# Moving row loads to GpSimd's queue, weight sums into the heads, and cover tiles across the gate pairs in a hybrid decoder layer

## The chip, the cores and the metric

The kernel runs on one core of one Trainium2 chip. The metric is the device time of one execution in microseconds (us), taken as the median of several runs. Each profile shows one execution. TensorE does the matmuls (PE in the profile, with its weight loads as PEld), VectorE is DVE, ScalarE is ACT, GpSimd is POOL, SyncE is SP. SP, ACT and POOL issue DMAs, and each of these queues is worked off in order.

## The reference

One layer of a decoder over 1024 tokens with 16 learned tokens ahead of them, in float32, model width 1024. Its mixing block projects the normalized input once and feeds two branches and two gates:

```python
proj = h @ w_in + b_in
(g_q, g_k, g_v, g_r, g_lr, m_q, m_k, m_v, m_o, m_i, m_f, gate_a, gate_b) = split(proj)
o_gla = head_rms(gla_chunked(g_q * dk**-0.5, g_k, g_v, log_a)) * silu(g_r)        # 4 heads
mq, mk = split(silu(causal_dwconv(concat(m_q, m_k))))
o_ml  = head_rms(mlstm_chunked(mq * dk**-0.5, mk, m_v, m_i, log_sigmoid(m_f))) * sigmoid(m_o)   # 4 heads
y = sigmoid(gate_a) * (o_gla @ w_branch_gla) + sigmoid(gate_b) * (o_ml @ w_branch_ml)
h = h + y @ w_out
u = causal_dwconv(rms_norm(h) @ w_up); gate, up = split(u)
h = h + (silu(gate) * up) @ w_down      # width 2816
out = rms_norm(h)[16:]
```

## The kernel before

Every float32 operand is split into a rounded high part and a low part (tile names end in H and L, or `wH`, `wL`), and a product is three matmuls: high by high, high by low, low by high. ACT makes the high part, DVE the low part. A weight tile of 512 KB takes one SP load into a raw buffer (two of them), one ACT copy and one DVE subtraction, in `prep` (L99 to L108), up to two tiles ahead of its use.

The kernel is a chain of stages. The order on each engine comes from a scheduler that takes the instructions in program order, shifted by priorities (`hp`), as its model of the time finds them ready; on the chip each engine and each queue then keeps that order.

*Heads* (`gla` and `mlstm`, L595 and L788). For s = 0 to 7 the projections of a head are the main work (`main`), and after each piece of a projection `advance` (L916) takes one step of the side work: the closing of a finished head (`post`, L544: scaling, transposes, norm, a store to `osc`) and the next step of the oldest open head. Between the fourth and the fifth head stands `small_rows` (L483), which prepares the gate rows of the second kind of head; each `yield` in it is one step. At the end of `post` of heads 3 to 6 `token_sums` (L459) builds four combinations of blocks of the normalized input on POOL and stores them to `tsc`. Heads 4 to 7 are the ones with convolutions. Tiles with the tag `gst` share one buffer.

*Tail and cover.* `merge_gate_b(j)` (L450) projects one 128-channel row block of the second merge gate with plain products and stores it to `gscb` from ACT's queue. Blocks 0, 1 and 2 (TAIL) run while the last head is closed. Block 3 (COVER) runs while `token_blocks` (L1059) loads the combinations and splits them.

*Pairs.* Thirteen pairs of row blocks (output gates of both branches, first merge gate, and the blocks of the second one that are left) are computed by `piece` (L960), two pieces each, with a Strassen-like scheme: seven products instead of eight, from the combinations and from sums of weight blocks. The results of a pair go into the row tiles `gu0` (tag `u0`, two buffers) and `gu1` (tag `u1`, one buffer). `gate_finish` (L1089) of the first eight pairs multiplies them with the heads' rows in `go` tiles (tag `o`, two buffers) and stores the product to `otd`; of the later pairs it stores the rows to `gsc` from ACT's queue. From pair 8 on (`q >= NK`), the two `o` buffers serve `half_sums`.

*Half sums.* The down projection at the end of the kernel also uses combinations of blocks of `w_down`. `half_sums` (L1103) makes one of 22 parts: two loads of 256 KB, four subtractions and two stores of 256 KB, all on POOL and its queue. Ten parts run in the pairs, five in the first branch (three after j = 1 in Y5 to Y7, two after j = 3 in Y6 and Y7), seven in the second (in Y0 to Y6).

*End tiles.* Blocks 6 and 7 of the second merge gate (END) run after the pairs as plain products.

*Branches.* The pool of the pairs is closed and `r2` takes its memory: a tile of `r2` waits for the old tiles that it lies on. `load_o` (L1162) loads eight rows of a branch's input (`ogL`, `omL`), and ACT and DVE split them (L1172, L1173). `merge_tile(j)` (L1201) loads a row of the first merge gate (`yg`) into Yj. All of it goes through SP's queue. `prod3` (L1181) multiplies: eight output blocks j for the GLA branch (`bg`), then eight for the mLSTM branch (`bm`), each of 72 matmuls into one of two groups of three PSUM banks; the first two `bg` blocks go row by row of the input as it arrives. DVE multiplies a block with the sigmoid of its gate (L1214), which frees the banks.

*Output projection and feed-forward.* `hacc` tiles h1 to h8 take the residual input in Y0 to Y7 (L1262 to L1268, all from SP); the products with `w_out` (`po`) are added to them (L1467). `hlo` (L1470) belongs to the two rows ahead of token 0. The rest of the kernel (second norm, up and down projection) is not touched.

Of the kernel before, what the change touches and what calls it, by code (L numbers as in the profile page):

```python
# [45 lines left out]
def hybrid_kernel(ctx, tc, x, meta, norm_mix, w_in, b_in, gla_w_gate, gla_b_gate, gla_norm,  # L46
# [167 lines left out]

    uk, uq, uv, ugb = {}, {}, {}, {}

    TAIL, COVER, END = (0, 1, 2), (3,), (6, 7)

    def head_units(s):
        h, g, k, q = s % 4, "gm"[s // 4], (O_GK, O_MK)[s // 4], (O_GQ, O_MQ)[s // 4]  # L220
# [149 lines left out]
    def cc(i):  # L370
        return col[:, i:i + 1]
# [99 lines left out]
            nc.sync.dma_start(tsc[i, k], src)  # L471


    raw_s = hd.tile([P, T], F32, name="raw_s", tag="raw", bufs=1)
    tcol = hd.tile([P, NC + 1, 4, 4], F32, name="tcol")

# [6 lines left out]
    def small_rows():  # L483
# [38 lines left out]
        nc.vector.tensor_tensor(d[:, :NM - 1], a[:, :NM - 1], M[:, NM - 2:NM - 1].to_broadcast([4, NM - 1]), OP.subtract)  # L522
        nc.scalar.activation(st[96:100, :NM - 1], d[:, :NM - 1], AF.Exp)
        nc.vector.memset(tcol[:, 0], 1.0)
        yield
        yield
        yield
        for g in range(3):
            tp = ps.tile([P, 4, P], F32, name=f"rtp{g}", tag="s", bufs=3)
            tq = tp.rearrange("p n (q w) -> p n q w", w=32)  # L530
# [13 lines left out]
    def post(s, o, om, sc, ncols):  # L544

        h = s % 4
        g = "g" if s < 4 else "m"
        for c in range(NC):
            nc.scalar.activation(o(c), o(c), AF.Copy, scale=sc[:, c + 1:c + 2])
        scaled = nc.scalar.activation(om, om, AF.Copy, scale=sc[:2, 0:1])  # L550
        for _ in range(3 if s != 3 else 5):
            yield
        for j in range(2):
            of = hd.tile([P, T], F32, name=f"of{s}_{j}", tag="r", bufs=2)
            for gi in range(2):
                tp = ps.tile([P, 4, P], F32, name=f"ot{s}_{j}_{gi}", tag="s", bufs=3)
                for i in range(4):
                    nc.tensor.transpose(tp[:, i, :], o(4 * gi + i)[:, j * P:(j + 1) * P], ident)
                a, b = 2 + 512 * gi, 2 + 512 * (gi + 1)
                nc.scalar.activation(of[:, a:b], tp.rearrange("p n w -> p (n w)"), AF.Copy, scale=ncols[j])  # L560
                if gi == 0:
                    yield
            tp = ps.tile([P, 4, P], F32, name=f"otm{s}_{j}", tag="s", bufs=3)
            nc.tensor.transpose(tp[:, 0, :2], om[:, j * P:(j + 1) * P], ident[:2, :2])
            nc.vector.tensor_scalar(of[:, 0:2], tp[:, 0, :2], ncols[j], None, OP.mult)
            nc.sync.dma_start(osc[g][2 * h + j], of[:, :NP])
            yield
        if 3 <= s < 7:
            with tc.issue_after(scaled.ins):
                token_sums(s - 3)  # L570

# [358 lines left out]
                advance()  # L930


    NP2 = NJ // 2
    tdn = [dram.tile([NP2, P, 2, 512], F32, name=f"tdn{i}") for i in range(2)]

    main(key_query_proj(0))
    decay(0)
    for s in range(8):
# [145 lines left out]
    def places():  # L1084

        for i in range(2):
            go[0, i] = row(f"go0_{i}", "o", 2)

    def gate_finish(q):  # L1089
        for i, u in enumerate(gu.pop(q)):  # L1090
            _, c, f, g, j = GATES[2 * q + i]
            if f is None:
                nc.scalar.dma_start(gsc[g][j], u[:, :NP])
                continue
            o = go[q, i] if q == 0 else row(f"go{q}_{i}", "o", 2)
# [5 lines left out]
    half = [(m, c) for m in range(NP2) for c in range(2)]  # L1101

    def half_sums(pool, tag, bufs=1):  # L1103
        m, c = half.pop(0)
        t = pool.tile([P, T], F32, name=f"ts{m}{c}", tag=tag, bufs=bufs)[:, :D].rearrange("p (i n) -> p i n", i=4)
        for k in range(2):
            nc.gpsimd.dma_start(t[:, 2 * k:2 * k + 2], w_dn[P * (2 * m + k):P * (2 * m + k + 1), :].rearrange(  # L1107
                "p (i n) -> p i n", i=2)[:, :, 256 * c:256 * c + 256])
        for o, a, b in ((0, 1, 0), (1, 3, 1), (3, 3, 0), (2, 2, 3)):
            nc.gpsimd.tensor_tensor(t[:, o], t[:, a], t[:, b], OP.subtract)  # L1110
        for i in range(2):
            nc.gpsimd.dma_start(tdn[i][m][:, :, 256 * c:256 * c + 256], t[:, 2 * i:2 * i + 2])
# [5 lines left out]
    with hp(PRI_W):  # L1118
        for _ in range(3):
            weights_step(0)  # L1120
    for j in COVER:
        main(merge_gate_b(j, gate_bank(f"pc{j}")))
    u2 = wp.tile([P, T], F32, name="gu2", tag="gst", bufs=1)[:, :2 * W0].rearrange("p (a b) -> p a b", b=W0)
    behind_ = None
    for q in range(NG):
        gu[q] = [row(f"gu{i}{q}", f"u{i}", 2 - i) for i in range(2)]
        for p in range(2):
            g = piece(psG, f"g{q}", p, gu[q], u2, WP[q], gate_block)
            next(g)
# [12 lines left out]
            next(g)  # L1142
            behind_ = g
        if q >= NK:
            for _ in range(2):
                half_sums(gs, "o", 2)
    next(behind_)
    for j in END:
        ugb[j] = u_cm(w_in, O_GB + P * j, f"gb{j}")
    gate_finish(NG - 1)  # L1150
    for i, j in enumerate(END):
        main(merge_gate_b(j, gate_bank(f"pe{j}"), row(f"gb{j}", "u0", 2) if i else None))
    gs_ctx.close()


# [3 lines left out]
    ps2_ctx = ctx.enter_context(ExitStack())  # L1159
    ps2 = ps2_ctx.enter_context(tc.tile_pool(name="ps2", bufs=1, space=PSUM, reuse_waits="tile"))  # L1160

    def load_o(g, pool, tags):  # L1162

        t = {}
        for p in "HL":
# [2 lines left out]
                t[p, i] = pool.tile(shape, F32R, name=f"o{g}{p}{i}", tag=tag)  # L1168
        for k in range(NK):
            h, l = (t[p, k // 4][:, k % 4, :NP] for p in "HL")  # L1170
            nc.sync.dma_start(l.bitcast(F32), otd[g][k])
            nc.scalar.activation(h, l.bitcast(F32), AF.Copy)  # L1172
            nc.vector.tensor_tensor(l, l.bitcast(F32), h.bitcast(F32), OP.subtract)  # L1173
        return tuple([t[p, k // 4][:, k % 4, :] for k in range(NK)] for p in "HL")
# [25 lines left out]

    def merge_tile(j):  # L1201
        yg.append(r2.tile([P, T], F32, name=f"yg{j}", tag=f"Y{j}")[:, :NP])
        nc.sync.dma_start(yg[j], gsc["a"][j])

    merge_tile(0)
    og = load_o("g", r2, "O")
    for j in range(NK):
        y = yg[j]
        if j < NK - 1:
            merge_tile(j + 1)  # L1210
        nc.scalar.activation(y, y, AF.Sigmoid, bias=cc(C_GA + j))
        pt = prod3(ubg[j], og, j < 2, f"bg{j}")
        with hp(PRI_E):
            merged = nc.vector.tensor_tensor(th(y), pt, th(y), OP.mult)  # L1214
        if j in (1, 3):
            with tc.issue_after(merged.ins):
                for i in (5, 6, 7) if j == 1 else (6, 7):
                    half_sums(r2, f"Y{i}")
    om_ = load_o("m", r1b, "R")

    yH = [r2.tile([P, NK, 2, 256], F32R, name=f"yH{i}", tag=f"OH{i}") for i in range(2)]
    yL = [r2.tile([P, NK, 2, 256], F32R, name=f"yL{i}", tag=f"OL{i}") for i in range(2)]
# [7 lines left out]
    for j in range(NK):  # L1230
# [17 lines left out]
                nc.scalar.activation(yh, z, AF.Copy)  # L1248
                nc.vector.tensor_tensor(yL[i][:, j], z, yh.bitcast(F32), OP.subtract)  # L1249
        if half:  # L1250
            half_sums(r2, f"Y{j}")
    r1b_ctx.close()
    ps2_ctx.close()
    psF = ctx.enter_context(tc.tile_pool(name="psF", bufs=1, space=PSUM, reuse_waits="tile"))
# [7 lines left out]
    for t in range(NC + 1):  # L1262
        a = r2.tile([P, T], F32, name=f"h{t}", tag=f"Y{t - 1}") if t else rb.tile([P, T], F32, name="h0", tag="T12")
        if t == 0:
            nc.sync.dma_start(a[:2, :D], meta[T0:NM, :])
        else:
            nc.sync.dma_start(a[:, :D], x[P * (t - 1):P * t, :])
# [545 lines left out]
```

## Time and profile before

| | |
|---|---|
| median of 3 runs | 1961.98 us (1961.19 to 1962.24) |
| the profiled execution | 1960.93 us, of which 1959.2 us span from the first to the last instruction |
| granted TensorE clock, mean | 0.985 |
| busy: PE, PEld, DVE, ACT, POOL | 96%, 91%, 61%, 44%, 19% |
| DMA | 270.03 MB, mean 138 GB/s |

The busy share of PE is a share of time in which some matmul was in flight. What a stage loses is seen in two ways: idle time ahead of an instruction with the operation that ended it, and the number of matmuls in a stretch against that in an undisturbed one, which counts a slower clock too. In the tables of stretches, the number behind x is how many instructions started in the stretch, and PEclk is the granted clock as a share of full speed.

### The profile page before, as it was taken

What the parts mean: (1) busy time and instruction counts of PE and PEld (TensorE: products, weight loads), DVE (VectorE), ACT (ScalarE), POOL (GpSimd) and SP (SyncE); (2) the same over time, 40 slices, a digit from 0 to 9 for tenths busy, and PEclk for the clock granted to TensorE, in tenths of its full rate; (3) what the DMA queues carried; (4) which work ended last, traced back from release to release, by engine and by line L of the source; (5) the groups of instructions that cost most, each with busy time, mean ns of one, the idle gap of its engine ahead of it and who ended that gap; (6) DMA issues with size and microseconds to landing.
All of it is one profiled execution on the core that took longest, in us unless ns stands there. A gap on an engine that the chain in (4) does not pass through costs nothing. (4 is left out here: it accounts for less than half of the span.)

```text
span 1959.2 us, 32654 instructions
## 1 busy us (share of the span) xinstructions
PE 1876.5 (96%) x13377; PEld 1791.5 (91%) x13377; DVE 1187.0 (61%) x1775; ACT 857.1 (44%) x1369; POOL 372.8 (19%) x405
## 2 busy tenths in 40 slices
PE   8999999899999999999679998999999999999998
PEld 8989989899999999999679998999999999987776
DVE  6555636644442666654331443688887878786776
ACT  5354554644454434322430223553434444355573
POOL 3101101122130010174330340002223222200000
PEclk9999999999999999999889999999999999999999
DMA  5111011142222675676861453333333333378794
GB/s 163 33 36 57 24 55 57 35 110 90 82 81 87 173 180 144 173 215 203 257 211 50 151 205 127 111 113 108 108 118 118 104 103 109 113 275 316 281 376 159
DMA packets 222593, 270.03 MB, mean 138 GB/s; under 512 B 13486, under 2 KB 176832, under 8 KB 222443
## 3 DMA queue, kind: packets, MB, share of 16 engines
q1 hardware_dynamic: 206651, 217.80, 35.6%
q0 software_dynamic: 11648, 39.89, 6.4%
q10 hardware_dynamic: 4144, 10.26, 1.4%
q8 instruction: 105, 1.72, 0.4%
q14 instruction: 45, 0.37, 0.1%
HBM read 198.33 MB, written 69.57 MB: 137 GB/s over the span
## 5 line engine op out<-in xcount | busy, mean ns | idle before, releaser
L1189 PE MATMUL bg<-ogH,wH_bg 128*128 128x342 f32 x192 | 63.3, 331 | 27.0 <-ACT ogH L1172 15.8
L1110 POOL TENSOR_TENSOR ts<-ts 128x256 f32<-128x256 f32 x88 | 73.7, 845 | 49.3 <-DMA ts<-in_ffn_w_down_dram 45.6
L1460 PE MATMUL po<-wH_wo,yH 128*128 128x256 f32 x256 | 73.9, 289 | 7.5 <-ACT hlo L1470 6.3
L1373 POOL TENSOR_TENSOR SB<-SA,rg 128x512 f32<-128x512 f32 x20 | 32.1, 1605 | 235.9 <-issue 114.1
L201 PE MATMUL pv<-wH_gv,xH 128*128 128x256 f32 x256 | 75.4, 294 | 0.0
L201 PE MATMUL pv<-wH_mv,xH 128*128 128x256 f32 x256 | 74.7, 292 | 0.1
L1460 PE MATMUL po<-wL_wo,yH 128*128 128x256 f32 x256 | 73.2, 287 | 0.9 <-DVE wL_wo L107 0.9
L1460 PE MATMUL po<-wH_wo,yL 128*128 128x256 f32 x256 | 73.0, 286 | 0.8 <-DVE yL L1249 0.8
L201 PE MATMUL pv<-wH_gv,xL 128*128 128x256 f32 x256 | 72.0, 281 | 0.0
L201 PE MATMUL pv<-wH_mv,xL 128*128 128x256 f32 x256 | 72.0, 281 | 0.0
L201 PE MATMUL pv<-wL_mv,xH 128*128 128x256 f32 x256 | 72.0, 281 | 0.0
L201 PE MATMUL pv<-wL_gv,xH 128*128 128x256 f32 x256 | 71.9, 281 | 0.0
L1408 DVE SCALAR_TENSOR_TENSOR cv<-u,fc,cv 128x1024 f32<-128x1024 f32 x44 | 65.3, 1484 | 0.4
L1189 PE MATMUL bg<-ogL,wH_bg 128*128 128x342 f32 x192 | 63.4, 332 | 1.1 <-DVE ogL L1173 1.1
L1107 POOL DMA_DIRECT2D ts<-in_ffn_w_down_dram x44 | 31.6, 723 | 167.2 <-DVE yM L1245 95.2
L1189 PEld LDWEIGHTS bg<-ogH,wH_bg 128*128 128x128 f32 x192 | 37.7, 197 | 27.5 <-ACT ogH L1172 16.1
L1189 PE MATMUL bg<-ogH,wL_bg 128*128 128x342 f32 x192 | 62.6, 327 | 0.0
L1355 POOL TENSOR_TENSOR A<-u2raw,A 128x512 fp32r<-128x512 f32 x20 | 43.9, 2194 | 92.9 <-ACT A L1354 92.9
L1189 PE MATMUL bm<-omH,wH_bm 128*128 128x342 f32 x192 | 61.4, 320 | 0.0
L1189 PE MATMUL bm<-omH,wL_bm 128*128 128x342 f32 x192 | 61.3, 319 | 0.0
L1189 PE MATMUL bm<-omL,wH_bm 128*128 128x342 f32 x192 | 61.2, 319 | 0.0
L675 POOL TENSOR_TENSOR pk<-pk,kT 128x256 f32<-128x256 f32 (+1 forms) x24 | 29.5, 1231 | 163.4 <-ACT pk L673 163.4
(747 smaller groups left out, 7436.0 us busy)
## 6 DMA issues: line engine op xcount, KB each, us to landing
gw<-in_w_in_dram SPq DMA_DIRECT2D x26, 512.0 KB
ts<-in_ffn_w_down_dram POOLq DMA_DIRECT2D x44, 256.0 KB, 5.2
tdn<-ts POOLq DMA_DIRECT2D x44, 256.0 KB, 2.6
rg<-in_ffn_w_up_dram SPq DMA_DIRECT2D x22, 512.0 KB
ru<-in_ffn_w_up_dram SPq DMA_DIRECT2D x22, 512.0 KB
adr<-s SPq DMA_DIRECT2D x40, 256.0 KB
rd<-in_ffn_w_down_dram SPq DMA_DIRECT2D x20, 512.0 KB
do<-tdn SPq DMA_DIRECT2D x18, 512.0 KB
```

Source lines behind the costliest of these rows:

```text
L201: nc.tensor.matmul(pt[:, :DV], a[:, k, t0:t0 + P], b[:, k % 4, :], start=(i == 0), stop=(i == 3 * NK - 1))
L675: eng.tensor_tensor(e, e, k, OP.mult)
L1107: nc.gpsimd.dma_start(t[:, 2 * k:2 * k + 2], w_dn[P * (2 * m + k):P * (2 * m + k + 1), :].rearrange("p (i n) -> p i n", i=2)[:, :, 256 * c ...
L1110: nc.gpsimd.tensor_tensor(t[:, o], t[:, a], t[:, b], OP.subtract)
L1189: nc.tensor.matmul(pt[:, i, :n], a[:, k, :], b[k][:, t0:t0 + n], start=(k == 0 and j == 0), stop=(k == NK - 1 and j == 2))
L1355: eng.tensor_tensor(l, src, h.bitcast(F32), OP.subtract)
L1373: late.tensor_tensor(sb[:, 0:4], sa[:, 0:4], rg[:, 0:4], OP.subtract)
L1408: nc.vector.scalar_tensor_tensor(y, u[:, j:SEQ + j], fc[:, j, jj:jj + 1], y, OP.mult, OP.add)
L1460: nc.tensor.matmul(pt[:, :DV], a, b[:, k % 4, :], start=(k == 0 and i == 0), stop=(k == NK - 1 and i == len(terms) - 1))
```

## The change

- Of `half_sums`, eight parts move into the heads: two at the end of `post(3)`, three each at the end of `post(4)` and `post(5)`, in the buffer `gst`. In the pairs six are left (two at pair 8, one at each later pair) in the one buffer `o0`; in the first branch three (after j = 1); in the second five, in Y0, Y1, Y2, Y2 and Y3.
- `small_rows` has six empty steps ahead of its transposes instead of three.
- COVER is blocks 3 and 4, END is block 7; blocks 5 and 6 go into the pairs. The number of pairs and of plain blocks stays the same. Block 4 uses a row of the tag `u0`, and so does block 7.
- The `o` buffers are named `o0` and `o1`; `gu1` of pairs 9 and 11 uses `o1`, so that from pair 8 on it has two buffers in turn.
- The loads of `og` and of all `yg` rows are issued from POOL's queue. The load of `om` stays on SP's, stands in the program behind block j = 1 of the first branch, and its ACT copies come behind the sigmoid of that block.
- h3, h4, h7 and h8 are loaded from POOL's queue.
- Two `issue_after` frames around POOL's work go away. They order only instructions on the named instruction's own engine, ACT or DVE, of which the framed work has none.

```diff
-    TAIL, COVER, END = (0, 1, 2), (3,), (6, 7)
+    TAIL, COVER, END = (0, 1, 2), (3, 4), (7,)
...
# small_rows
-        yield
-        yield
-        yield
+        for _ in range(6):
+            yield
...
# post
         if 3 <= s < 7:
-            with tc.issue_after(scaled.ins):
-                token_sums(s - 3)
+            token_sums(s - 3)
+            for _ in range((2, 3, 3, 0)[s - 3]):
+                half_sums(wp, "gst")
...
# places, gate_finish: rows "o" (2 buffers) become "o0" and "o1"
-            go[0, i] = row(f"go0_{i}", "o", 2)
+            go[0, i] = row(f"go0_{i}", f"o{i}")
...
-    for j in COVER:
-        main(merge_gate_b(j, gate_bank(f"pc{j}")))
+    for i, j in enumerate(COVER):
+        main(merge_gate_b(j, gate_bank(f"pc{j}"), row(f"gb{j}", "u0", 2) if i else None))
...
     for q in range(NG):
-        gu[q] = [row(f"gu{i}{q}", f"u{i}", 2 - i) for i in range(2)]
+        gu[q] = [row(f"gu0{q}", "u0", 2), row(f"gu1{q}", "o1" if q >= NK and q % 2 else "u1")]
...
         if q >= NK:
-            for _ in range(2):
-                half_sums(gs, "o", 2)
+            for _ in range(2 if q == NK else 1):
+                half_sums(gs, "o0")
...
-    for i, j in enumerate(END):
-        main(merge_gate_b(j, gate_bank(f"pe{j}"), row(f"gb{j}", "u0", 2) if i else None))
+    for j in END:
+        main(merge_gate_b(j, gate_bank(f"pe{j}"), row(f"gb{j}", "u0", 2)))
...
-    def load_o(g, pool, tags):
+    def load_o(g, pool, tags, queue):
...
-            nc.sync.dma_start(l.bitcast(F32), otd[g][k])
+            queue.dma_start(l.bitcast(F32), otd[g][k])
...
     def merge_tile(j):
-        nc.sync.dma_start(yg[j], gsc["a"][j])
+        nc.gpsimd.dma_start(yg[j], gsc["a"][j])

     merge_tile(0)
-    og = load_o("g", r2, "O")
+    og = load_o("g", r2, "O", nc.gpsimd)
     for j in range(NK):
...
-        nc.scalar.activation(y, y, AF.Sigmoid, bias=cc(C_GA + j))
+        opened = nc.scalar.activation(y, y, AF.Sigmoid, bias=cc(C_GA + j))
         pt = prod3(ubg[j], og, j < 2, f"bg{j}")
         with hp(PRI_E):
-            merged = nc.vector.tensor_tensor(th(y), pt, th(y), OP.mult)
-        if j in (1, 3):
-            with tc.issue_after(merged.ins):
-                for i in (5, 6, 7) if j == 1 else (6, 7):
-                    half_sums(r2, f"Y{i}")
-    om_ = load_o("m", r1b, "R")
+            nc.vector.tensor_tensor(th(y), pt, th(y), OP.mult)
+        if j == 1:
+            with tc.issue_after(opened.ins):
+                om_ = load_o("m", r1b, "R", nc.sync)
+            for i in (5, 6, 7):
+                half_sums(r2, f"Y{i}")
...
         if half:
-            half_sums(r2, f"Y{j}")
+            half_sums(r2, f"Y{j if j < 3 else 3 - j % 2}")
...
-            nc.sync.dma_start(a[:, :D], x[P * (t - 1):P * t, :])
+            (nc.gpsimd if t in (3, 4, 7, 8) else nc.sync).dma_start(a[:, :D], x[P * (t - 1):P * t, :])
```

More of the change, by code (lines that the diff above doesn't have):

```diff
@@ L471, in token_sums, with half_sums @@
             nc.sync.dma_start(tsc[i, k], src)
+    NP2 = NJ // 2
+    tdn = [dram.tile([NP2, P, 2, 512], F32, name=f"tdn{i}") for i in range(2)]
+    half = [(m, c) for m in range(NP2) for c in range(2)]
+    def half_sums(pool, tag, bufs=1):
+        m, c = half.pop(0)
+        t = pool.tile([P, T], F32, name=f"ts{m}{c}", tag=tag, bufs=bufs)[:, :D].rearrange("p (i n) -> p i n", i=4)
+        for k in range(2):
+            nc.gpsimd.dma_start(t[:, 2 * k:2 * k + 2], w_dn[P * (2 * m + k):P * (2 * m + k + 1), :].rearrange(
+                "p (i n) -> p i n", i=2)[:, :, 256 * c:256 * c + 256])
+        for o, a, b in ((0, 1, 0), (1, 3, 1), (3, 3, 0), (2, 2, 3)):
+            nc.gpsimd.tensor_tensor(t[:, o], t[:, a], t[:, b], OP.subtract)
+        for i in range(2):
+            nc.gpsimd.dma_start(tdn[i][m][:, :, 256 * c:256 * c + 256], t[:, 2 * i:2 * i + 2])
     raw_s = hd.tile([P, T], F32, name="raw_s", tag="raw", bufs=1)
@@ L549, in post @@
             nc.scalar.activation(o(c), o(c), AF.Copy, scale=sc[:, c + 1:c + 2])
-        scaled = nc.scalar.activation(om, om, AF.Copy, scale=sc[:2, 0:1])
+        nc.scalar.activation(om, om, AF.Copy, scale=sc[:2, 0:1])
         for _ in range(3 if s != 3 else 5):
@@ L930, in main @@
                 advance()
-    NP2 = NJ // 2
-    tdn = [dram.tile([NP2, P, 2, 512], F32, name=f"tdn{i}") for i in range(2)]
     main(key_query_proj(0))
@@ L1094, in gate_finish @@
                 continue
-            o = go[q, i] if q == 0 else row(f"go{q}_{i}", "o", 2)
+            o = go[q, i] if q == 0 else row(f"go{q}_{i}", f"o{i}")
             nc.gpsimd.dma_start(o[:, :NP], osc[g][j])
@@ L1099, in gate_finish @@
             nc.gpsimd.dma_start(otd[g][j], o[:, :NP])
[L1101 to L1112, printed above, removed]
     def gate_bank(name):
```

## The prediction, made before the changed kernel was run

> **What bounds the kernel now.** I read the page first, then the waits of TensorE, then stretches around the longest of them, then the queues in those stretches.
>
> ```profile
> span 1959.2 us, 32654 instructions
> PE 1876.5 (96%) x13377; PEld 1791.5 (91%) x13377; DVE 1187.0 (61%) x1775; ACT 857.1 (44%) x1369; POOL 372.8 (19%) x405
> ```
> ```profile
> PE bg L1189 <- ACT ogH L1172: 15.8, 1, 15.8
> PE bg L1189 <- DVE yg L1214: 11.2, 1, 11.2
> PE po L1460 <- ACT hlo L1470: 6.3, 1, 6.3
> PE Yg L957 <- DVE gu L985: 6.3, 5, 3.0
> PE rtp L534 <- ACT of L560: 4.9, 1, 4.9
> ```
>
> TensorE is the bound: it works 96% of the span, and no matmul is added or taken away by the change. So only its gaps can move, and five groups of waits (total, times, longest) make up most of them. Next, the same places as stretches of time, with two undisturbed ones (985 to 1010 and 1195 to 1210) as the measure.
>
> ```profile
> 385.00:395.00 10.00, 5.08 (x28) 4.65 (x27) 8.31 (x19) 7.61 (x9) 0.10 (x1) 0.83 0.61 173
> 400.00:590.00 190.00, 189.39 (x1314) 178.45 (x1313) 88.87 (x196) 88.67 (x177) 47.75 (x31) 1.00 0.30 86
> 865.00:880.00 15.00, 12.03 (x79) 11.83 (x78) 5.45 (x9) 2.87 (x5) 10.56 (x14) 0.77 0.90 220
> 945.00:980.00 35.00, 18.16 (x97) 16.48 (x97) 16.46 (x13) 17.96 (x18) 16.69 (x20) 0.76 0.96 317
> 985.00:1010.00 25.00, 25.00 (x160) 25.00 (x159) 1.23 (x1) 2.99 (x3) 11.88 (x17) 1.00 0.62 197
> 1010.00:1030.00 20.00, 8.75 (x42) 8.51 (x41) 13.04 (x11) 9.56 (x10) 0.00 (x0) 0.66 0.64 223
> 1180.00:1195.00 15.00, 8.69 (x52) 8.58 (x52) 2.55 (x5) 2.96 (x8) 0.00 (x0) 0.77 0.56 175
> 1195.00:1210.00 15.00, 15.00 (x127) 14.83 (x127) 5.06 (x9) 4.71 (x13) 0.00 (x0) 1.00 0.23 71
> ```
>
> The columns are length, busy time of PE, PEld, DVE, ACT and POOL with the number of instructions, PEclk, DMA share and GB/s. Undisturbed, branch matmuls start at 160/25 = 6.4 per us and the smaller ones at 127/15 = 8.47. What a stretch loses is its length less its matmuls over that rate:
>
> - A, 945 to 980: 35 − 97/6.4 = 19.8 us (15.8 of it idle, the rest slow clock and pacing by arriving rows).
> - B, 1010 to 1030: 20 − 42/6.4 = 13.4 us (11.2 idle).
> - C, 1180 to 1195: 15 − 52/8.47 = 8.9 us (6.3 idle).
> - D, 385 to 395: 10 − 28/8.47 = 6.7 us (4.9 idle).
> - E, 865 to 880: 15 − 79/8.47 = 5.7 us (3.0 idle).
>
> Together 54.5 us. A gap costs more than its idle time: PEclk is 0.66 to 0.83 in these stretches and 1.00 in the others.
>
> **A: the first branch waits for its input.** SP's queue in order of time, and the wait inside the `ogL` issues:
>
> ```profile
> 946.76 0.81 SPq L1171 DMA_DIRECT2D omL<-otdm  x2
> 948.95 0.38 SPq L102 DMA_DIRECT2D wr_bg<-in_w_branch_gla_dram  x1
> 949.39 1.18 SPq L1203 DMA_DIRECT2D yg<-gsca  x1
> 950.74 9.68 SPq L1171 DMA_DIRECT2D ogL<-otdg  x8
> 961.38 36.55 SPq L1203 DMA_DIRECT2D yg<-gsca  x6
> 998.03 0.38 SPq L102 DMA_DIRECT2D wr_bg<-in_w_branch_gla_dram  x1
> ```
> ```profile
> SPq L1171 <- PE pe L158: 4.7, 1, 4.7
> ```
> ```profile
> SPq L1171 <- DMA gscb<-gb: 4.4, 1, 4.4
> ```
> ```profile
> 961.39 1.06 ACT L1172 ACTIVATE ogH<-ogL 128x1026 fp32r<-128x1026 f32 x1
> ```
> ```profile
> 974.47 1.06 ACT L1172 ACTIVATE ogH<-ogL 128x1026 fp32r<-128x1026 f32 x1 [0.59 <-DMA ogL<-otdg]
> ```
>
> Two loads for the second branch stand ahead of the first branch's and wait 4.7 us for the last end tile, until 946.76; the `og` loads follow at 950.74, and half of them wait another 4.4 us for the store of block 7. Their splits run from 961.39 to 974.47, so a row takes (974.47 − 961.39)/7 = 1.9 us at a DMA share of 0.96.
>
> After the change the `og` loads stand in POOL's queue behind nothing but the last half sum and one `yg` row, and wait for what really holds their memory. The combinations lie there, and they are last read by the last pair; one end tile, 72/6.4 = 11.3 us, runs after that. An early load thus has 11.3 us of cover. The nearest load from POOL's queue is that of a `go` row, of the same size:
>
> ```profile
> ts<-in_ffn_w_down_dram POOLq DMA_DIRECT2D x44, 256.0 KB, 5.2
> go<-oscg POOLq DMA_DIRECT2D x8, 513.0 KB, 5.5
> ```
>
> 5.5 us to land, 1.06 to split on ACT and an estimated as much on DVE: the first row is ready about 8 us after the last pair, ahead of 11.3. The eighth is ready at 8 + 7 × 1.9 = 21; TensorE, going row by row at 9/6.4 = 1.4 us each, wants it at 11.3 + 7 × 1.4 = 21.1. So the loss of A falls between 0 and, where half the rows still lie under the row of block 7, about 12 (the eight issues above are spread over 9.68 us by that wait, and the `om` loads share the DMA engines then). I keep 5: A gives **14.8 us**.
>
> One rule speaks against this part. The Trainium skill, "Trainium Kernel Development and Optimization", Key Constraints, says that DMAs from all queues share the same 16 engines, and that issuing from several saves only the sequencer's issue time. Issue time here is 0.81/2 = 0.4 us a load, eight of them 3.2 us, and by that rule A would give about 3 us. The rows disagree: `og` lost 4.7 us to another load's wait ahead of it in an ordered queue, which is not issue time.
>
> **B: rows of the merge gate behind the half sums.** Between the two `wr_bg` issues SP hangs on `yg` rows until 998.03 (the x6 row lasts 36.55 us). What holds it, and what ACT then waits for:
>
> ```profile
> SPq L1203 <- DMA tdn<-ts: 22.9, 4, 7.1
> ```
> ```profile
> 1001.87 1.15 ACT L1211 ACTIVATE yg<-yg,col 128x1026 f32<-128x1026 f32 x1 [17.03 <-DMA yg<-gsca]
> ```
>
> Rows 5 to 7 reuse the buffers of five half sums and wait for their stores; weights and `om` queue up behind them, ACT stands 17.03 us, and DVE can't free a bank. After, three half sums stand there instead of five, and the wait is in POOL's queue with no weights behind it. POOL's in-order queue does hold `yg3` to `yg7` behind three sums; a sum's period is
>
> ```profile
> 1098.18 1.44 POOL L1107 DMA_DIRECT2D ts<-in_ffn_w_down_dram  x2 [2.40 <-ACT yM L1244]
> ```
> ```profile
> 1112.00 1.44 POOL L1107 DMA_DIRECT2D ts<-in_ffn_w_down_dram  x2 [1.83 <-DVE yM L1245]
> ```
>
> 13.8 us with one buffer, so at most 41 us if no sum overlaps another. Block 5 needs its row 5 × 11.3 = 56 us after the branch starts, block 3 at 34. B should vanish; I keep 1 of the 13.4: **12.4 us**.
>
> **C: the output projection's second weights.** SP at the end of the second branch, and ACT:
>
> ```profile
> SPq L1267 <- DMA tdn<-ts: 12.8, 3, 9.3
> ```
> ```profile
> 1179.06 0.34 SPq L1267 DMA_DIRECT2D h<-in_x_dram  x1
> 1179.56 0.68 SPq L102 DMA_DIRECT2D wr_wo<-in_w_out_dram  x1
> ```
> ```profile
> 1184.91 1.06 ACT L106 ACTIVATE wH_wo<-wr_wo 128x1024 fp32r<-128x1024 f32 x1 [6.18 <-DMA wr_wo<-in_w_out_dram]
> ```
>
> An `h` load waits for the half sum in Y6, and the weights stand behind it. The change ends the sums at j = 4, none lies in Y4 to Y6, and the late `h` loads leave SP's queue. I keep 1: **7.9 us**.
>
> **D and E.** Three more empty steps, about 3/1.15 pieces of a projection (24 matmuls, 24/8.47 = 2.8 us each), stand ahead of the transposes that wait 4.9 us: their inputs are there by then. The steps push the later heads back by as much, and the second cover tile (11.3 us) takes that up at the end. I keep 1: **5.7 us**. In E, DVE waits for the store of the single `u1` buffer:
>
> ```profile
> DVE gu L985 <- DMA gsca<-gu: 7.8, 3, 3.5
> ```
>
> With two buffers from pair 8 on this has no place to come from: **5.7 us**.
>
> **What is added.** Eight half sums in the heads: about 8 × 13.8 = 110 us of POOL's time (its DMA waits included) in a stage where POOL works 47.75 of 190 us. They are hidden by TensorE's own work, 189.39 of 190. What they could hold up is POOL's small work for the heads (the roots for the scaling, the memsets of the convolutions) and the buffer `gst`. The three sums of head 5 fall between two of `token_sums`:
>
> ```profile
> 541.92 1.28 POOL L469 TENSOR_TENSOR xb<-xb,tx 128x514 f32<-128x514 f32 x1
> ```
> ```profile
> 580.82 1.30 POOL L469 TENSOR_TENSOR tx<-xa 128x514 f32<-128x514 f32 x1
> ```
> ```profile
> 599.52 0.46 ACT L453 ACTIVATE gb<-pj 128x342 f32<-128x342 f32 x1 [2.11 <-issue]
> ```
>
> That is 38 us for 3 × 13.8 = 41; with the shift of D some 10 us are left until the tail's first row needs `gst` at 599.52. The cost lies between 0 and 15 us (a wait in each of three heads at 5.2 us); nearest is the fully busy row 400 to 590, so I take **5 us**. Six sums in one `o0` take 6 × 13.8 = 83 us of the five last pairs (5 pairs of 168 matmuls at 8.47 per us, 99 us): hidden, and the last one leaves POOL's queue before `og` wants it.
>
> Sum: −14.8 − 12.4 − 7.9 − 5.7 − 5.7 + 5 = −41.5 us. On the profiled execution, 1960.93, that is 1919.4; the median of the runs is 1 us higher, so 1920.
>
> **Rivals.**
>
> R1, the loads come no earlier: the scheduler may put the half sums ahead of the rows in POOL's queue, or half the rows still wait for block 7's store. For it: the 4.4 us wait on exactly that store. Against: only half the rows waited. A then gives nothing: 1920 + 15 = 1935. A second mechanism would take half as much: each of the eight issues on POOL held for one split on DVE, 8 × 1.06 = 8 us, which gives 1928; I give it 0.03 of R1's chance, since `go` rows land in 5.5 us from that queue. The Trainium skill, "SBUF — State Buffer", Who interferes with whom, states it as a rule: a DMA issued from GpSimd's queue can be starved of descriptors while DVE holds the port that both use.
>
> R2, slower: the half sums in the heads. Each holds POOL until its load has landed, 5.2 us; if a root or a memset stands behind it, ACT and then TensorE stop, and the clock falls. C shows the price of falling: 8.9 − 6.3 = 2.6 us. Eight such gaps cost 8 × 7.8 = 62 us in place of the 5 above: 1920 − 5 + 62 = 1977. It decides the sign from 46.5/7.8 = 6 of the eight on. Against it: ACT works 88.67 of 190 us there, and TensorE lost 0.6 us in all.
>
> R3, the order on the queues comes out such that gaps of the same size open elsewhere (`yg` behind the sums, `om` beside `og`): no change, 1962.
>
> **How the numbers follow.** About 0.2% (4 us) is what a measurement can tell from no change. Likeliest case 0.62, its own range 1906 (nothing kept, nothing added: 1961 − 54.5) to 1934; R1 0.15, 1934 to 1945; between R1 and no change 0.08, where the heads cost their 15 us and A gives nothing; R3 0.05; R2 0.10. Faster is 0.62 + 0.15 + 0.08 = 0.85. The range to 1952 leaves out R2, R3 and a little of the case between.
>
> **What the profile would show.** Right: `og` issues on POOL's queue ahead of the end of block 7, and the wait of `bg` for `ogH` under 6 us; no wait of `bg` for `yg`; no wait for `hlo` and `rtp`; no DVE wait for `gsca` stores after pair 8; PE as full as now between 400 and 590. Wrong: `ts` ahead of `ogL` in POOL's queue; `omL` loads landing among the `ogL`; waits of ACT for `rs4r` to `rs6r` with TensorE idle; the tail's `gb` row waiting for `tdn` or `tsc` stores.

## The result: slower by 0.9%, where a gain of 2% was predicted

The changed kernel takes 1979.39 us (median of 4 runs, 1976.76 to 1985.01) beside 1962.11 for the kernel before on the same chip (4 runs): a ratio of 1.0093, 95% interval 1.007 to 1.0115. The predicted 1920 would have been a ratio of 0.979. The profiled execution took 1985.01 us, the slowest of the four.

The head of the page and TensorE's waits of the changed kernel (total, times, longest):

```profile
span 1983.3 us, 32663 instructions
PE 1883.7 (95%) x13377; PEld 1799.7 (91%) x13377; DVE 1196.9 (60%) x1775; ACT 853.8 (43%) x1369; POOL 390.9 (20%) x425
```
```profile
PE ot L572 <- ACT or L563: 28.6, 2, 15.2
PE bg L1188 <- ACT ogH L1171: 24.3, 2, 16.6
PE Xg L969 <- DVE gu L989: 8.2, 1, 8.2
...
PE op L902 <- DVE dn L905: 3.4, 2, 2.7
```

The number of matmuls is the same. Of the waits that the prediction counted, those of `bg` for `yg`, of `po` for `hlo`, of `rtp` and of `Yg` for `gu` are gone from the list. New are 28.6 us of `ot`, the transposes at the end of a head; the wait at the start of the pairs has grown from 1.9 to 8.2, and `bg` waits more for `ogH`, not less (24.3 against 15.8). The stretches that answer to those of before (same columns; the first line is 600 to 650 in the kernel before):

```profile
600.00:650.00 50.00, 50.00 (x312) 48.80 (x311) 10.90 (x27) 19.44 (x47) 3.06 (x3) 1.00 0.37 104
```
```profile
400.00:590.00 190.00, 172.90 (x1161) 162.76 (x1161) 93.34 (x187) 78.54 (x160) 81.06 (x76) 0.96 0.40 111
...
600.00:650.00 50.00, 41.62 (x251) 37.33 (x252) 15.04 (x37) 17.63 (x40) 15.11 (x12) 0.86 0.23 74
...
985.00:1000.00 15.00, 0.00 (x0) 0.00 (x0) 1.23 (x1) 4.87 (x7) 0.00 (x0) 0.52 0.82 306
1000.00:1022.00 22.00, 13.89 (x62) 12.96 (x63) 8.95 (x8) 8.92 (x11) 11.95 (x17) 0.73 0.90 305
```

The stretch 400 to 590, the undisturbed measure of the prediction, now holds 1161 matmuls instead of 1314: 153/6.92 (1314 over 190 us) is 22 us lost. From 600 to 650 it is 251 instead of 312, which at 312/50 = 6.24 per us is another 10 us. TensorE does nothing at all from 985 to 1000.

The chain of stages can be followed by the first and the last start of the first product of each stage (min, median and max duration in ns, then first and last start in us). First the kernel before, then the changed one:

```profile
L957 PE MATMUL Vg<-xH,gHA x104: 277/281/287, 650.1 to 911.0; 128*128 128x258 f32 x52, 128*128 128x256 f32 x52
L1189 PE MATMUL bg<-ogH,wH_bg x192: 312/319/655, 962.5 to 1070.6; 128*128 128x342 f32 x192
L1460 PE MATMUL po<-wH_wo,yH x256: 276/281/581, 1161.7 to 1279.5; 128*128 128x256 f32 x128
L957 PE MATMUL Vu<-BH,HA x64: 278/281/364, 1280.6 to 1687.7; 128*128 128x258 f32 x64
L1609 PE MATMUL pdX<-do,dy x108: 387/394/404, 1749.4 to 1943.9; 128*128 128x512 f32 x108
```
```profile
L969 PE MATMUL Vg<-xH,gHA x104: 277/281/418, 700.2 to 959.2; 128*128 128x258 f32 x52, 128*128 128x256 f32 x52
L1188 PE MATMUL bg<-ogH,wH_bg x192: 312/319/655, 1000.1 to 1103.2; 128*128 128x342 f32 x192
L1459 PE MATMUL po<-wH_wo,yH x256: 276/281/388, 1194.3 to 1299.7; 128*128 128x256 f32 x128
L969 PE MATMUL Vu<-BH,HA x64: 278/281/365, 1300.8 to 1709.1; 128*128 128x258 f32 x64
L1608 PE MATMUL pdX<-do,dy x108: 387/394/404, 1773.8 to 1968.3; 128*128 128x512 f32 x108
```

Differences of these starts, with the cover tile (11.3 us) that moved from behind the pairs to ahead of them taken out; the last column is a version shown further down, e12:

| stage | predicted | changed kernel | e12 |
|---|---|---|---|
| all up to the first pair, less 11.3 | −0.7 (D −5.7, added +5) | +38.8 | +1.6 |
| the pairs | −5.7 (E) | −1.9 | −2.9 |
| last pair to first `bg`, plus 11.3 | −14.8 (A) | +0.7 | −12.2 |
| `bg` blocks | −12.4 (B) | −5.0 | −15.2 |
| `po` | −7.9 (C) | −12.4 | −12.5 |
| `Vu` to the last `pdX` | 0 | +4.2 | −0.2 |
| to the last `pdX` | −41.5 | +24.4 | −41.3 |

(What is left between the rows is below 0.2 us.) The changed kernel's column is that of its slowest run, so its total of +24.4 is more than the 17 us between the medians. So the loss sits in the heads and in front of the first branch. In the heads, POOL's order in the changed kernel:

```profile
500.98 1.51 POOL L482 DMA_DIRECT2D ts<-in_ffn_w_down_dram  x2 [0.30 <-POOL xb L469]
...
515.06 1.44 POOL L482 DMA_DIRECT2D ts<-in_ffn_w_down_dram  x2 [2.39 <-DMA tdn<-ts]
...
525.88 1.44 POOL L482 DMA_DIRECT2D ts<-in_ffn_w_down_dram  x2 [2.39 <-DMA tdn<-ts]
...
533.26 1.92 POOL L93 TENSOR_TENSOR rs5r<-rs5v,mhalf 128x9 f32<-128x9 f32 x1
```

Three half sums stand one after the other in one buffer, and behind them the root that scales head 5. ACT in order of time (the bracket is the idle time ahead and what ended it):

```profile
535.42 3.30 ACT L563 ACTIVATE or<-or,rs5r 128x256 f32<-128x256 f32 x8 [20.62 <-DVE rs5r L916]
...
605.16 3.30 ACT L563 ACTIVATE or<-or,rs6r 128x256 f32<-128x256 f32 x8 [20.43 <-DVE rs6r L916]
...
994.73 1.15 ACT L1235 ACTIVATE sb<-sb,col 128x1026 f32<-128x1026 f32 x1 [18.27 <-DMA sb<-gscb]
...
998.97 5.78 ACT L1171 ACTIVATE ogH<-ogL 128x1026 fp32r<-128x1026 f32 x6
...
1017.83 1.15 ACT L1235 ACTIVATE sb<-sb,col 128x1026 f32<-128x1026 f32 x1 [13.08 <-DMA sb<-gscb]
1018.89 1.99 ACT L1171 ACTIVATE ogH<-ogL 128x1026 fp32r<-128x1026 f32 x2
```

The first two rows are the 20 us that ACT stands for a root, twice. The last four are the branch. The splits of `og` come six and two in a row, so their rows had landed. What they stand behind is the sigmoid of `sb0` and `sb1`, rows of the *second* merge gate that only the second branch needs. ACT waits 18 and 13 us for their loads. In the kernel before, the sigmoid of `sb0` came well ahead of the splits, which began at 961.39, and waited little:

```profile
945.22 1.15 ACT L1236 ACTIVATE sb<-sb,col 128x1026 f32<-128x1026 f32 x1 [1.79 <-DMA sb<-gscb]
```

In the changed kernel the load of `sb0` was issued, in SP's queue, at

```profile
974.86 0.62 SPq L1234 DMA_DIRECT2D sb<-gscb  x1
```

and its sigmoid starts 20 us later, while eight `og` rows and the branch's weights use the DMA engines.

### The profile page after: what moved, and what is told of

It reads as the page before. It is cut to its first block, busy times and chain, and to the rows that moved or that the text cites. A ratio compares the mean times of both kernels' runs of the same rounds, so it can differ in the third digit from the quotient of the medians.

```text
span 1983.3 us, 32663 instructions
## 1 busy us (share of the span) xinstructions
PE 1883.7 (95%) x13377; PEld 1799.7 (91%) x13377; DVE 1196.9 (60%) x1775; ACT 853.8 (43%) x1369; POOL 390.9 (20%) x425
## 5 line engine op out<-in xcount | busy, mean ns | idle before, releaser
L1188 PE MATMUL bg<-ogH,wH_bg 128*128 128x342 f32 x192 | 63.2, 330 | 24.3 <-ACT ogH L1171 24.3
```

What stands on the lines that cost most here:

```text
L1188: nc.tensor.matmul(pt[:, i, :n], a[:, k, :], b[k][:, t0:t0 + n], start=(k == 0 and j == 0), stop=(k == NK - 1 and j == 2))
```

## Experiments

Four theories. **T1**: the root of a head stands behind three half sums in POOL's order. **T2**: the rows of the second merge gate stand ahead of the `og` splits in ACT's order. **T3**: two cover tiles hold up the weights of the first pair. **T4**: the tail's first row waits for the buffer `gst`, which the last `token_sums` gives back too late. Rivals stand in the expectations. Ratios are against the kernel before on the same chip, with their 95% intervals; a point is 0.01 of the ratio, some 20 us.

**e1_roots_first.** T1 alone: the eight sums behind the roots, two at each of heads 3 to 6.

```diff
-            for _ in range((2, 3, 3, 0)[s - 3]):
-                half_sums(wp, "gst")
...
# called right after post(s, ...) has been opened; root[0] is the power on POOL
+    def sums_after_root(s):
+        if 3 <= s < 7:
+            with tc.issue_after(root[0].ins):
+                for _ in range((2, 2, 2, 2)[s - 3]):
+                    half_sums(wp, "gst")
```

> The changed kernel, with the eight half sums of the heads placed behind the root of the head's scaling on GpSimd instead of behind the head's closing: two each behind the roots of heads 3 to 6, ordered so by hand. Theory 1 (the three sums of heads 4 and 5 stand in GpSimd's queue ahead of the next root, ScalarE waits 20.6 and 20.4 us for it, TensorE 15.2 and 13.4): both waits go, and with the slow clock behind them 30 to 38 us come back, near 1945 us. Rival (the six empty steps, or the shared buffer gst, delay the heads whatever the order of the sums): 1970 to 1985 us, with TensorE still idle between 500 and 660.

Measured: 1954.92 us, ratio 0.9976 [0.9964, 0.9989]. TensorE's waits:

```profile
PE bg L1196 <- ACT ogH L1179: 24.1, 2, 16.0
PE op L909 <- DVE dn L912: 8.8, 2, 7.8
```

The waits of `ot` for `or` are gone (ACT's at the roots of heads 5 and 6 fall to 1.2 and 2.9 us), the one of the branch is as in the changed kernel, and `op` now waits 7.8 us in the tail, where it waited at most 2.7. The first pair starts at 674.1 instead of 700.2: this order is worth 26 us there, net of the new wait, and 1.17 points or 23 us of the whole. That is less than the 30 to 38 that were expected, but far from the rival's 1970 and more.

**e2_gate_rows_behind.** T2 alone: the first two sigmoids of `sb` are ordered behind the last split of `og`.

```diff
-            nc.scalar.activation(h, l.bitcast(F32), AF.Copy)
+            split_of[g] = nc.scalar.activation(h, l.bitcast(F32), AF.Copy)
...
-        nc.scalar.activation(sb, sb, AF.Sigmoid, bias=cc(C_GB + j))
+        with tc.issue_after(split_of["g"].ins) if j < 2 else nullcontext():
+            nc.scalar.activation(sb, sb, AF.Sigmoid, bias=cc(C_GB + j))
```

> The changed kernel, with ScalarE's sigmoids of the first two rows of the second branch's gate (sb) ordered behind the last split of the first branch's input. Theory 2 (the loads on GpSimd's queue land in time, but ScalarE stands 18.3 and 13.1 us at those two sigmoids, whose loads come late, with the splits behind them): the two waits of the first branch for ogH, 24.3 us, fall below 6 and 20 to 27 us come back, near 1955 us. Rival (the rows themselves land late from GpSimd's queue, starved or contended): the waits move to the splits and under 8 us come back, 1971 us or more.

Measured: 1956.38 us, ratio 0.9985 [0.9973, 0.9997].

```profile
PE ot L572 <- ACT or L563: 27.6, 2, 14.6
...
PE bg L1190 <- ACT ogH L1173: 3.9, 1, 3.9
```

The branch's wait falls from 24.3 to 3.9, the heads' stays. An order of two activations on ACT was worth 1.08 points, 21 us.

**e3_both_orders.** Both edits.

> The changed kernel with both orders, sums behind the roots and gate rows behind the splits. If both theories hold and the losses add: near 1920 us, some 2% below the kernel before. If the one only uncovers the other: 1940 to 1960 us.

Measured: 1929.52 us, ratio 0.9852 [0.9824, 0.988]. The two gains, 1.17 and 1.08 points, add up to 2.25; together they give 2.41. T1 and T2 are separate losses. The time itself lies between the two that were expected (near 1920, and 1940 to 1960), because gaps are left:

```profile
PE bg L1198 <- ACT ogH L1181: 10.2, 1, 10.2
PE op L909 <- DVE dn L912: 8.1, 2, 7.3
PE Xg L977 <- DVE gu L997: 6.0, 2, 5.5
```
```profile
ACT gb L455 <- DMA tsc<-tx: 13.4, 1, 13.4
```

The 10.2 us of `bg` are those of one execution, the slowest of the four (1937.37 us). There ACT stood 9.57 us, from 952 to 961.77, for a late weight of the branch (`wr_bg`) that comes ahead of the splits in its order; in e7, e9 and e12, with the same two orders, `bg` waits 3.9.

**e4_three_steps.** A rival to T1: the three added steps of `small_rows` bring the sums ahead of the roots.

```diff
-        for _ in range(6):
+        for _ in range(3):
             yield
```

> The changed kernel with three empty steps ahead of the transposes of the gate rows, as before, instead of six. Theory 1: the sums still hold the roots, so TensorE still waits at the transposes of heads 4 and 5, and the time stays between 1970 and 1990 us; the wait at the gate rows' transposes (4.9 us before) comes back. Rival (the later steps push the heads into the sums): 1945 to 1960 us.

Measured: 1978.7 us, ratio 1.0097 [1.0078, 1.0116].

```profile
ACT or L563 <- DVE rs5r L916: 18.9, 1, 18.9
ACT or L563 <- DVE rs6r L916: 18.2, 1, 18.2
```

ACT's waits stay, and the wait of `rtp` comes back with its old 4.9 us. TensorE stands 12.1 us at one `ot` and 14.5 us at a `pv` that waits for ACT, instead of at two `ot`. The steps are not the cause, and they do take away the wait that the prediction said (D).

**e5_sums_alone.** The other way round: the kernel *before* with the eight sums in the heads (2, 3, 3) and nothing else; the ten of the pairs stay, the branch keeps four, the second branch has none.

```diff
# in the kernel before
             with tc.issue_after(scaled.ins):
                 token_sums(s - 3)
+            for _ in range((2, 3, 3, 0)[s - 3]):
+                half_sums(wp, "gst")
...
-                for i in (5, 6, 7) if j == 1 else (6, 7):
+                for i in (5, 6, 7) if j == 1 else (6,):
```

> The kernel before with one part of the change alone: eight half sums at the end of post of heads 3 to 5 in gst (2, 3, 3). The ten sums of the pairs and three of the first branch stay, one more follows there, and the second branch has none. T1 (three sums in POOL's order ahead of a root cost the heads 20 us at each of two roots): ACT or <- DVE rs5r and rs6r of 18 to 21 us each, first pair 20 to 30 us later than before, while B and C give back up to 9 + 9 us: 1965 to 1985. Rival T1b (it takes the three added steps of small_rows as well, or the new cover tiles, to put the sums ahead of the roots): no such wait, and a time of 1945 to 1960.

Measured: 1980.78 us, ratio 1.0087 [1.0065, 1.0109].

```profile
ACT or L565 <- DVE rs6r L919: 22.8, 1, 22.8
ACT or L565 <- DVE rs5r L919: 18.9, 1, 18.9
```

T1 holds without any other part of the change; its rival falls. The time is in the expected range, but the first pair starts at 691.0, 41 us later than before and not 20 to 30. The output projection (`po`) is as short here as in the changed kernel, 105.4 us from its first to its last start against 117.8 before, though all `h` loads are still in SP's queue.

**e6_sp_queue.** Is it the queue that brings `og` early? The version e3 with `og` and `yg` back on SP (both are moved, so the run does not tell them apart).

```diff
-    og = load_o("g", r2, "O", nc.gpsimd)
+    og = load_o("g", r2, "O", nc.sync)
...
-        nc.gpsimd.dma_start(yg[j], gsc["a"][j])
+        nc.sync.dma_start(yg[j], gsc["a"][j])
```

> The kernel after with both orders (sums behind the roots, gate rows of the second merge gate behind the last og split), but the og and yg loads issued from SP's queue again. If the queue is what brings og early (the prediction's part A), bg waits for ogH 10 to 16 us more, and yg behind the half sums holds the weights on SP: 1940 to 1955, slower than the 1930 of the version with both orders by 10 us or more. Rival (the Trainium skill, Trainium Kernel Development and Optimization, Key Constraints: only issue time is saved by another queue): within 4 us of that version. Third: sb0, the weights and om then stand behind og on SP instead of beside it, which brings og earlier: faster than it by up to 8 us.

Measured: 1945.7 us, ratio 0.9913 [0.9887, 0.9939], 0.61 points or 12 us behind e3 (with both intervals taken together, some 4 to 19). The issues of `og` in e3 (POOL's queue), and in e6 (SP's):

```profile
939.75 2.10 POOL L1180 DMA_DIRECT2D ogL<-otdg  x4 [3.21 <-ACT gu L1004]
945.36 2.09 POOL L1180 DMA_DIRECT2D ogL<-otdg  x4 [3.51 <-PE Zg L977]
```
```profile
962.53 9.40 SPq L1180 DMA_DIRECT2D ogL<-otdg  x8
```

The last pair's first product started at 930 in e3 and at 934 in e6, so on SP the rows come some 19 us later, behind two `om` loads that wait for the last end tile, and `bg` waits 15.7 us. Within that width, the queue is worth what A was priced at.

**e7_three_orders** and **e10_one_cover** are for T3. e7 is e3 with the second halves of the split combinations ordered behind the first pair's weights on ACT; e10 is e3 with the old cover.

```diff
# e7
+    with tc.issue_after(last_split[0].ins):    # the third weight of the first pair
+        split_blocks(slice(W0, 514))
# e10
-    TAIL, COVER, END = (0, 1, 2), (3, 4), (7,)
+    TAIL, COVER, END = (0, 1, 2), (3,), (6, 7)
```

> The kernel after with both orders and a third: the second halves of the split combinations (TH) come behind the split of the first pair's third weight on ACT. T3 (the two cover tiles hold the weight slots, so that the first pair's second weights are split behind the TH splits, which wait for their own load): the wait of Xg for DVE gu and the gap at the pairs' start of 8 us in the kernel after (5.5 idle in the version with both orders) go to under 1, and the kernel gains 4 to 8 us against that version: 1922 to 1926. Rival (the weights' own loads are late): the wait stays, 1928 to 1932.

> The version with both orders, with the cover as it was: block 3 alone ahead of the pairs, blocks 6 and 7 behind them. T3 (two cover tiles hold the weight slots that the first pair's weights need): the third gw load no longer waits 18.6 us in SP's queue, the wait of Xg for DVE gu falls from 5.5 to 2 or less, 3 to 6 us faster. Against it, T3b: with one cover tile TensorE reaches the pairs 11.3 us earlier, the combinations are not split yet, and the gap opens ahead of the first Vg or stays at Xg, so that nothing is gained: within 3 us. Third: the second end tile gives og 11.3 us more of cover, and the wait of bg for ogH (10.2) goes: up to 8 us more.

Measured: e7 1932.54 us, ratio 0.9848 [0.9829, 0.9866]; e10 1930.17 us, ratio 0.9848 [0.9827, 0.9869]; both the same as e3. In e7 ACT stands for the weight itself:

```profile
678.61 1.06 ACT L1035 ACTIVATE gHA<-gw 128x1024 fp32r<-128x1024 f32 x1 [9.08 <-DMA gw<-in_w_in_dram]
```

and `Xg` still waits 7.1 us; the order on ACT was not the cause. In e10 the wait of `Xg` falls to 2.7, and the time doesn't move. T3 is right on the place and worth nothing in sum, as its rival in e10 had it (T3b, a gain within 3 us). That `og` would gain from the longer cover did not show: `bg` waits 6.1 us for it.

**e8_early_roots_three_orders.** For T4: e7 with the sums at the roots of heads 3 to 5 (2, 3, 3), so that the last `token_sums` comes earlier.

```diff
-                for _ in range((2, 2, 2, 2)[s - 3]):
+                for _ in range((2, 3, 3, 0)[s - 3]):
                     half_sums(wp, "gst")
```

> As the version with three orders, but the sums stand behind the roots of heads 3, 4 and 5 (2, 3, 3) instead of 3 to 6 (two each), so that the last of them and the last token_sums come earlier and gst is free for the tail's first row. T4 (the tail's row waits for gst): ACT gb <- DMA tsc<-tx of 13 us and op <- DVE dn of 7 to 8 us go, 5 to 9 us faster than the version with three orders: 1914 to 1919. Rival (three sums behind one root are still ahead of the next head's root): ACT waits for rs5r and rs6r come back, 5 to 20 us each, and the time is 1925 to 1945.

Measured: 1943.02 us, ratio 0.9905 [0.988, 0.993]: slower than e7 by 0.57 points. The time is in the rival's range, but its waits are not there: the roots are on time with three sums behind them, so in T1 it is the order that counts. `op` waits 2.2 us at the longest instead of 8.2, as T4 has it, but there is a new wait of 9.7 us of `pv` in the heads. SP's longest wait from 520 to 600, SP's queue, and DVE:

```profile
SPq L473 <- POOL tx L471: 37.5, 2, 29.0
```
```profile
575.83 0.39 SPq L818 DMA_DIRECT2D WB<-rsc  x1
```
```profile
582.29 0.17 DVE L841 COPY gp<-WB 128x8 f32<-128x8 f32 x1 [13.17 <-DMA WB<-rsc]
```

Three sums make the next `token_sums` late; SP stands 29 us at its store, and behind the store is the load `WB` for the last head (at 555.70 in e7). The same fault as T1, handed on through a second queue.

**e9_earlier_heads**, **e12_tail_row** and **e13_tail_row_one_cover.** T4 without that side effect: e9 is e3 with two sums at the roots of heads 2 to 5; e12 is e3 with another buffer for the tail's first and third row; e13 is e12 with the old cover.

```diff
# e9
-    if 3 <= s < 7:
+    if 2 <= s < 6:
# e12, e13
     for j in TAIL:
-        main(merge_gate_b(j))
+        main(merge_gate_b(j, None, None if j % 2 else hd.tile([P, T], F32, name=f"gb{j}", tag="bc")))
```

> The version with both orders, but the sums stand behind the roots of heads 2 to 5 (two each) instead of 3 to 6: none is left behind the last token_sums. T4 (the tail's first row waits for gst, because the sums of head 6 push the last token_sums to 591 to 607): ACT gb <- DMA tsc<-tx of 13 us and op <- DVE dn of 7 us go, 5 to 9 us faster than the version with both orders, 1921 to 1926. Rival (the sums of head 2 find gst held by the decay rows of head 3, and POOL stands behind them): waits of ACT or DVE for POOL's work between 290 and 400, and no gain or up to 10 us lost, 1930 to 1940.

> The version with both orders, in which the first and third row of the tail get a buffer of their own (that of the decay rows, long free by then) instead of gst. T4: ACT gb <- DMA tsc<-tx of 13 us and op <- DVE dn of 7 us are gone, with the clock's part 6 to 10 us faster than the version with both orders: 1920 to 1925. Rival (the wait of op comes from elsewhere, such as the head's own chain on ACT and DVE): op <- DVE dn stays over 5, and the time stays within 3 us.

> Both of the last two together: own rows for the tail, and the cover as it was. If the two gaps are separate, the gains add up: 10 to 15 us faster than the version with both orders, 1915 to 1922, where the prediction put the change. If one gap only shifts into the other (the pairs' start is bound by the transfers of the combinations, which wait for the same token_sums), the two together gain no more than the tail's row alone: 1921 to 1926.

Measured: e9 1923.88 us, ratio 0.9823 [0.9797, 0.985]; e12 1921.1 us, ratio 0.9799 [0.9774, 0.9825]; e13 1921.59 us, ratio 0.9802 [0.9783, 0.9821]. TensorE's waits in e12, and its splits of `og`:

```profile
PE Xg L977 <- DVE gu L997: 7.3, 1, 7.3
PE bg L1198 <- ACT ogH L1181: 3.9, 1, 3.9
```
```profile
947.92 7.88 ACT L1181 ACTIVATE ogH<-ogL 128x1026 fp32r<-128x1026 f32 x8
```

The wait of `op` has fallen to 0.8 and that of ACT for `tsc` is gone, and the first pair starts at 663.0 instead of 673.4. In e9 both waits only fall, to 3.0 and 8.3, and the gain over e3 is 0.29 points. T4 holds; it was worth 0.53 points, 10 us (e10 against e13, on one chip with separate intervals, gives 0.46). With the old cover (e13) nothing is won or lost: the pairs, 255.0 us from the first to the last start, are 3.0 shorter than in e12, but the first pair loses 1.2 and the way from the last pair to the first `bg` 2.2, each with the moved cover tile taken out. e12 beats the kernel before by 2.0%, and its stages are the last column of the table above:

```profile
L977 PE MATMUL Vg<-xH,gHA x104: 277/281/415, 663.0 to 921.0; 128*128 128x258 f32 x52, 128*128 128x256 f32 x52
L1198 PE MATMUL bg<-ogH,wH_bg x192: 312/319/491, 949.0 to 1041.9; 128*128 128x342 f32 x192
L1470 PE MATMUL po<-wH_wo,yH x256: 276/281/389, 1133.0 to 1238.3; 128*128 128x256 f32 x128
L977 PE MATMUL Vu<-BH,HA x64: 278/281/368, 1239.5 to 1646.5; 128*128 128x258 f32 x64
L1619 PE MATMUL pdX<-do,dy x108: 388/394/404, 1708.0 to 1902.6; 128*128 128x512 f32 x108
```

## Why the prediction was wrong

The predicted sign was wrong. The working fails at two of its steps, and both are about the order on one engine.

**The added sums, +5 with bounds 0 to 15: failed.** The sentence "nearest is the fully busy row 400 to 590, so I take 5 us" took TensorE's full stretch and POOL's idle share there as cover. It set the upper bound by one landing (5.2 us) in each of three heads. But three sums stand in a row, in one buffer, so that each waits for the store of the one before: POOL is held from 500.98 to the root at 533.26, 32 us, and the root is wanted some 20 us before that. The price is 20.6 and 20.4 us of ACT's wait, and 15.2 and 13.4 of TensorE's; e1 and e5 show the cause, and in e1 the first pair starts 26 us earlier. The margin of `gst` for the tail's first row (T4) was named but not counted. Its 10 us (e12 against e3) belong to the versions with two sums at head 6, where `op` waits 7 to 8 us; in the changed kernel it waits 2.7. With both gone (e12) the first stage stands at +1.6 instead of +38.8, where −0.7 was predicted; if D gave its 5.7, the sums cost about 7 us there.

**A, 14.8 us: right on the queue, failed on ACT's order.** The loads came early, and `og` stood ahead of the sums in POOL's queue, as predicted; yet the way from the last pair to the first `bg` changed by +0.7 instead of −14.8 us. The working timed load, split and matmul, and never asked what else ACT has in its order at that place. In the kernel before, the sigmoid of `sb0` waits 1.79 us, ahead of the splits; in the changed kernel it is the 18.27 us row. "Half the rows landing late" or `om` among `og` (the items listed as signs) did not decide it. With T1, T2 and T4 mended (e12), the way to the first `bg` measures −12.2, and the wait left over is 3.9 us. Up to 4 of A's 19.8 us lay behind the first `bg` (at 962.5), in the next row of the table, so A and B are better taken together: 27.2 predicted, 27.4 in e12.

**B, 12.4 us: right, hidden by T2.** No wait of `bg` for `yg` is left. The `bg` blocks gain only 5.0, since the last two `og` splits stand behind `sb1` (13.08 us); 15.2 in e12, with a part of A in it.

**C, 7.9 us: right, too small.** `po` gains 12.4 in the changed kernel and 12.5 in e12. In e5, which takes the sums out of the second branch and leaves the `h` loads on SP, it gains 12.4 too: the sums did it, not the queue of the `h` loads. **D, 5.7 us: right on the wait**, by e4; what it is worth in time is not shown (1.0097 without it, 1.0093 with it, while the heads wait for their roots). By the heads' own rate, 6.92 per us, the working's loss there would be 10 − 28/6.92 = 6.0 us, not 6.7. **E, 5.7 us: the wait is gone, the gain is not all there.** The pairs are 1.9 us shorter (2.9 in e12), since the wait at their start grew to 7 to 8 us (T3), which no step of the prediction had. With the old cover (e13), where that wait is 2.4, they are 5.9 shorter, about as predicted.

That e12's total of −41.3 meets the predicted −41.5 so closely is in part luck: C gave 4.6 us more than predicted, E 2.8 less and the first stage 2.3 less.

**The rivals.** R2, at 0.10, had the mechanism: roots behind sums, ACT, then TensorE. Its price was wrong in both factors: not eight gaps of 7.8 us, of which six would turn the sign, but two that idled TensorE for 15.2 and 13.4 us, because sums in a row add up ahead of one root. That its 1977 is close to the measured 1979 is luck: the heads cost less than its 62 us, and A, which it kept, was lost. R1 has the right size for A (nothing gained) by the wrong way: the `og` loads were issued from 968.86 to 975, ahead of the three half sums of the branch, and held neither by the store of block 7 (issued at 997.54) nor by splits on DVE (from 1000.0). R3 came true in part: gaps of the same size did open elsewhere, but at the sigmoids of `sb`, not at `yg` or `om`. Of the signs that the working listed for being wrong, ACT's waits for `rs5r` and `rs6r` are there, and the tail's `gb` row waits 8.7 us for a `tsc` store.

The two rules that were weighed for A can be told apart now. The Trainium skill, "Trainium Kernel Development and Optimization", Key Constraints, states a rule with two halves. That all queues share the same engines agrees with the landing of `og` in the changed kernel, 14.0 us in the median, beside 5.2 for a `go` row of the same size. That another queue saves issue time only does not agree with e6: 12 us (at least some 4), where eight issues are 3.2 us. The difference is what stands ahead in the queue. Of the starvation that the Trainium skill describes in "SBUF — State Buffer", Who interferes with whom, no trace here shows a cost: in e12 eight splits follow each other without a wait for a row that POOL's queue had loaded.

One thing stays open. In the profiled execution of the changed kernel the stretch from `Vu` to the last `pdX` is 4.2 us longer than before. No other version shows more than 2.5 us (e13), and the other three runs of it were 4.6 to 8.3 us shorter; the cause is not known.

## What to carry to other kernels

Work that is put on a half-idle engine costs nothing only if nothing short and urgent stands behind it in that engine's order; so list, for each place where it is inserted, the next instruction that another engine waits for, and count what stands ahead of that one in a row, with its DMA waits. When a load is made earlier, go through the order of *every* engine on its path: a consumer that is ready early can still stand behind something for a later stage. And put such work behind the urgent instruction by an order of its own: here two orders and one buffer turned +0.9% into −2.0%.

## What the runs showed of the hardware

A load of 513 KB took from 5 us to about 20 us until its consumer could start, by what was under way beside it: 5.2 us for `go`, 14.0 in the median for `og` behind each other, and some 20 for `sb0`, issued at 974.86 in a stretch with a DMA share of 0.98 (968 to 985) and 0.82 (985 to 1000). A stretch of 15 us with no matmul at all had a granted clock of 0.52, and the next one of 22 us only 0.73, while 1.00 was granted in the kernel before from 400 to 590, where TensorE was busy for 189.39 of 190 us.
